# A hybrid decoder block: 32 tokens of the expert stage move from the dense path to the gathered path

## The chip, the core and the metric

The kernel runs on one core of a Trainium2 chip. The metric is the time of one execution on the device in microseconds (us), the median over several runs. TensorE (PE) multiplies, with its weight loads shown as PEld; VectorE (DVE), ScalarE (ACT) and GpSimd (POOL) do the elementwise work; SyncE (SP) issues the plain transfers; POOL issues the indirect ones. Each engine works through its own instructions in a fixed order that is settled when the kernel is compiled.

## What is computed

One decoder layer over 1024 tokens of width 1024: a combined projection, a gated DeltaNet and a sliding-window attention, an output projection, then PEER (retrieval of single-neuron experts), then a gated per-layer embedding and a final norm. The change touches PEER alone:

```
qry   = (ht @ wq)                        # 8 heads, two halves of 128
top_s, top_i = top_k(qry . sub_keys, 16)
best_s, expert = the 16 best of the 256 sums, per head   # 128 experts per token
gates = softmax(best_s)
act   = gelu(sum_d h[t, d] * u_tab[expert[t, k], d])
y[t]  = sum_k gates[t, k] * act[t, k] * v_tab[expert[t, k]]
```

There are 16384 experts; each token uses 128 of them (8 heads of 16).

## The kernel before

The tokens are cut into 8 blocks of 128. Their experts are computed in two ways, side by side in time.

**Dense path** (`DBLK`, blocks 0 to 4, 640 tokens; `dense`, from L922). All 16384 experts are multiplied with all tokens of these blocks, in 128 chunks `c` of 128 experts. For a chunk, `prepared` loads `ur` and `vr` and splits each into a high and a low part (`uh`, `ul`, `vh`, `vl`; ACT takes the high part, DVE the low one). Then, for each of two parts of 320 tokens, 8 x 3 matmuls fill a bank `bk_u` (tag "u", 2 banks); ACT turns it into `ge` (L988), DVE multiplies it with the gate table `Gt`, ACT and DVE split the product into `wh` and `wl`. After 4 chunks (one `cg`, 32 of them), the second product follows: for each of the 5 blocks and 2 halves of the width, 12 matmuls of 512 columns. Blocks 0 and 1 keep their sums in four banks "yp" through the whole stage; blocks 2 to 4 use the tag "y" with 2 banks, taken in turn, and DVE adds each bank to `xB` before the bank is free again. The gate table in DRAM (`gd`) was written earlier by `gbuild`.

**Gathered path** (`ABLK`, blocks 5 to 7; `gather_block`, L874). One partition is one token. For each of the 128 slots, POOL issues an indirect DMA (`fetched`, L858) that brings one row of `u` for each of 128 tokens, and DVE forms the dot product with `h2n` (`gather_dots`, L868). After the gelu, 128 more slots bring rows of `v`, and DVE adds each, scaled, to `acc` (L82). The landing tiles `rows` are a ring of 7 (`GBUF` 4 and `GXBUF` 3). The three blocks have 3 x 2 x 128 = 768 such steps.

What sets the order of the two: `step` in `dense` is called after each chunk and each (block, half), 448 times, and lets the gather job emit its share of the steps; `held_back` ties each gather instruction on DVE behind the third-last such point. Beyond that, a scheduler places the instructions of each engine by its own model when the program is built.

**Final stage** (`final`, L1002): per block a norm, eight transposes and 48 matmuls of 512 columns on `bk_g`, a gate, a last norm and the store, in the order 5, 6, 0, 1, 2, 3, 4, 7. Blocks 5 to 7 are read back from `x1d`, where the gathered path leaves them.

Of the kernel before, what the change touches and what calls it, by code (L numbers as in the profile page):

```python
# [7 lines left out]
F32 = mybir.dt.float32  # L8
# [22 lines left out]
ABLK = [5, 6, 7]  # L31
UBLK = HBLK + ABLK
BBLK = HBLK + DBLK
NU = len(DBLK) * 128
GC = 4
TB = 16
GBUF = 4
# [30 lines left out]
def block_kernel(ctx: ExitStack, tc, I, out, dbg=None):  # L68
    nc = tc.nc
    V, S, G, PE = nc.vector, nc.scalar, nc.gpsimd, nc.tensor  # L70
    NB = len(BBLK)
    NT = NB * P
    NH = len(HBLK) * P

    def copy(o, i, **k):
# [36 lines left out]

    ident = cp.tile([P, P], F32, name="ident")
    iota = cp.tile([P, P], F32, name="iota")
    sel_b = cp.tile([P, 3, 16, 8], BF, name="sel_b")
    mhalf = cp.tile([P, 8], F32, name="mhalf")
    G.memset(mhalf, -0.5)
# [10 lines left out]
    def load_consts():  # L128
        nc.sync.dma_start(ident, I["consts"][:, 0:P])
        nc.sync.dma_start(iota, I["consts"][:, 4 * P:5 * P])  # L130
        nc.sync.dma_start(cst, I["consts"][:, P:])
        V.tensor_copy(sel_b.rearrange("p s a h -> p (s a) h"), bc(sel[:, 58:106], 2, 8))
        V.memset(negt, NEG)
# [249 lines left out]
    def retrieving(lt, es):  # L383
# [14 lines left out]
        def retrieve(gi):  # L398
# [26 lines left out]
            for bi, b in enumerate(grp):  # L425
                xt = xts[bi]
                bs_ = slice(bi * P, (bi + 1) * P)
                nc.sync.dma_start(x1d[b], xt)
                h = norm(sm, "h", xt, ffnw, 1)
                if b in UBLK:  # L430
                    nc.sync.dma_start(h2d[UBLK.index(b)], h)
                transpose_split("s3", h, h2h, h2l, bs_)
                if b in DBLK:
                    t0 = (b - DBLK[0]) * P
                    nc.sync.dma_start(h2Td[0][:, :, t0:t0 + P], h2h.bitcast(F32)[:, :, bs_])
                    nc.sync.dma_start(h2Td[1][:, :, t0:t0 + P], h2l.bitcast(F32)[:, :, bs_])
            tv = [lt.tile([P, 16, 16], F32, tag="tv", name="tv", bufs=2) for _ in grp]
            tiu = [lt.tile([P, 16, 16], U32, tag="tiu", name="tiu", bufs=2) for _ in grp]
            for q4 in range(4):
# [317 lines left out]
    def topk(tk, bg, b, v, iu):  # L757
# [61 lines left out]
            stt(eidx[:, UBLK.index(b)], i1, 128.0, i2, ALU.mult, ALU.add)  # L819
        if b in ABLK:  # L820
            return
        pt = bank("gm", [4, P])
        tr(pt[:, 0], i1)
        tr(pt[:, 1], i2)
# [11 lines left out]

    def gbuild(bg, b):
        tT = slots[b]
        for tb in range(P // TB):
            stage = bg.tile([P, NE, TB], F32, tag="stage", name="stage", bufs=2)  # L840
            for t0 in range(0, TB, 4):
                c0 = tb * TB + t0
                o12 = bg.tile([P, 2, 4, P], F32, tag="o12", name="o12", bufs=2)
                o1, o2 = o12[:, 0], o12[:, 1]
                tt(o12, bc(bc(iota, 1, 4), 1, 2), bc(tT[:, 0:2, c0:c0 + 4], 3, P), ALU.is_equal)
                for i in range(4):
                    copy(o2[:, i], o2[:, i], scale=tT[:, 2, c0 + i:c0 + i + 1])
                pg = bank("gm", [4, P])
                for i in range(4):
                    mm(pg[:, i], o2[:, i], o1[:, i])  # L850
                copy(stage[:, :, t0:t0 + 4], pg.rearrange("p t e -> p e t"))
                yield
            nc.sync.dma_start(gd[:, :, BBLK.index(b) * (P // TB) + tb].rearrange("g p c t -> p g (c t)"),
                              stage.rearrange("p (g c) t -> p g (c t)", c=GC))

    def fetched(gp, tab, u, s):
        r = (pools["gx"] if "gx" in pools and s % 2 else gp).tile([P, D], F32, tag="rows", name="rows")
        G.indirect_dma_start(out=r, out_offset=None, in_=tab,  # L858
                             in_offset=bass.IndirectOffsetOnAxis(ap=eidx[:, u, s:s + 1], axis=0))
        return r  # L860

    def gather_dots(gp, u):
# [38 lines left out]
    pools = {}  # L901
    credit = [0.0]

    def gather_job():
        for b in ABLK:
            yield from gather_block(pools["gp"], b)

# [16 lines left out]
    def dense(xB):  # L924
        with ExitStack() as es:
# [12 lines left out]
            nparts = (NU + 511) // 512  # L938
            width = (NU // nparts + TB - 1) // TB * TB
            parts = [(n0, min(width, NU - n0)) for n0 in range(0, NU, width)]  # L940
            total = len(ABLK) * 2 * P
            steps = NE + NE // GC * NB * 2
            count = [0, 0]
            pools["job"] = gather_job()
# [22 lines left out]
            for cg in range(NE // GC):  # L967
# [30 lines left out]
                for bi in range(NB):  # L998
                    for j in range(2):
# [2 lines left out]
                        py = held[bi, j] if keep else bank("y")  # L1002
                        for ci in range(GC):
                            (vh, vl), (wh, wl) = vs[ci], ws[ci]
                            ts_ = slice(bi * P, (bi + 1) * P)
                            mm3(py, wh[:, ts_], wl[:, ts_], vh[:, cs], vl[:, cs],
                                ci == 0 and (cg == 0 or not keep), ci == GC - 1 and (cg == NE // GC - 1 or not keep))
                        if not keep or cg == NE // GC - 1:
                            last = tt(xB[:, bi, cs], py, xB[:, bi, cs], ALU.add)
                        step(last)  # L1010
            drain()

# [64 lines left out]
def _host(inputs):  # L1077
# [8 lines left out]
    wo_s = wo[512:].reshape(2, 4, 64, 1024).transpose(1, 0, 2, 3).reshape(512, 1024)  # L1086
    d = {
        "consts": _consts(),
        "x": a["x"][0],
        "pos": a["positions"][0].reshape(8, 128).T,  # L1090
        "mix_norm": a["mix_norm"][0],
# [42 lines left out]
```

## Time and profile before

| | |
|---|---|
| median of 3 runs (lowest, highest) | 3034.56 us (3032.35, 3036.15) |
| the profiled execution | 3043.6 us, span 3041.8 us |
| PE busy in the span | 2936.2 us, 97% |
| DVE busy | 2499.4 us, 82% |
| ACT busy, POOL busy | 1234.6 us, 1068.4 us |
| HBM read, written | 766.40 MB, 99.61 MB |
| moved by POOL's queue | 402.70 MB |

The span runs from the first to the last instruction. "Busy" is the time in which at least one instruction of the engine is under way; for PE the instructions overlap, so that what a matmul costs is read from the distance between two starts and not from its duration. "PEclk" is the granted clock of TensorE as a share of 2.4 GHz; "DMA share" is the mean busy share of the core's 16 DMA engines.

### The profile page before, as it was taken

The numbers are of one execution on the slowest core, as the hardware profiler recorded it, in microseconds if no ns is written. First come the engines' busy times: TensorE is split into PE (matmuls) and PEld (weight loads), VectorE is DVE, ScalarE is ACT, GpSimd is POOL, SyncE is SP. The second block draws the span as 40 slices with busy tenths as digits, with TensorE's granted clock in tenths as the row PEclk, the third lists the DMA queues.
The fourth block names the chain that finished last, engine by engine and source line by source line (L and its number), as shares of the span: only waits on it lengthen the run. The fifth ranks groups of instructions, "written<-read, shape, count | busy, mean of one in ns | idle before, by whom it ended". The sixth has DMA issues, their size and how long they took to land. (4 is left out here: it accounts for less than half of the span.)

```text
span 3041.8 us, 49726 instructions
## 1 busy us (share of the span) xinstructions
PE 2936.2 (97%) x18287; PEld 2690.0 (88%) x18287; DVE 2499.4 (82%) x5023; ACT 1234.6 (41%) x2761; POOL 1068.4 (35%) x901
## 2 busy tenths in 40 slices
PE   7999999999999889999999999999999999999988
PEld 5887999999998789999999989998898898998967
DVE  5658636898999779988699889887998898899974
ACT  5556634488777663222222222232232232222223
POOL 0000000000000000765356556554656565556541
PEclk9989999999999999999999999999999999999989
DMA  7569657689889994999799989888999899899962
GB/s 236 142 223 364 206 191 248 215 223 243 237 242 270 287 279 141 351 338 348 272 342 354 330 319 369 329 332 300 335 351 345 318 358 332 306 337 347 324 256 89
DMA packets 449955, 869.30 MB, mean 286 GB/s; under 512 B 193456, under 2 KB 235824, under 8 KB 445360
## 3 DMA queue, kind: packets, MB, share of 16 engines
q1 hardware_dynamic: 339120, 463.43, 46.5%
q0 software_dynamic: 110592, 402.70, 36.4%
q8 instruction: 143, 2.34, 0.3%
q14 instruction: 100, 0.82, 0.1%
HBM read 766.40 MB, written 99.61 MB: 285 GB/s over the span
## 5 line engine op out<-in xcount | busy, mean ns | idle before, releaser
L136 PE MATMUL bk_u<-hT,uh 128*128 128x320 f32 x4096 | 915.4, 310 | 7.0 <-DMA hT<-h2Td 3.7
L136 PEld LDWEIGHTS bk_u<-hT,uh 128*128 128x128 f32 x4096 | 695.7, 189 | 23.2 <-ACT ge L988 4.6
L858 POOL DMA_INDIRECT rows<-in_u_dram,eidx x384 | 499.1, 1300 | 555.5 <-DVE dots L868 283.1
L136 PE MATMUL bk_u<-hT,ul 128*128 128x320 f32 x2048 | 635.0, 310 | 0.3 <-DVE ul L79 0.3
L858 POOL DMA_INDIRECT rows<-in_v_dram,eidx x384 | 498.6, 1298 | 350.1 <-DVE acc L82 287.5
L82 DVE SCALAR_TENSOR_TENSOR acc<-rows,dots,acc 128x1024 f32<-128x1024 f32 x384 | 492.2, 1282 | 35.4 <-DMA rows<-in_v_dram,eidx 24.5
L868 DVE CUSTOM_DVE_ANT_0 rows<-rows,h2n 128x1024 f32<-128x1024 f32 x384 | 459.9, 1223 | 27.5 <-DMA rows<-in_u_dram,eidx 27.3
L136 PEld LDWEIGHTS bk_u<-hT,ul 128*128 128x128 f32 x2048 | 386.5, 189 | 4.1 <-DVE ul L79 0.7
L988 ACT ACTIVATE ge<-bk_u 128x320 f32<-128x320 f32 x256 | 109.8, 431 | 603.3 <-PE bk_u L136 552.6
L136 PE MATMUL bk_y<-vh,wh 128*128 128x512 f32 x768 | 298.9, 391 | 3.0 <-DVE xB L79 3.0
L136 PE MATMUL bk_y<-vl,wh 128*128 128x512 f32 x768 | 299.9, 392 | 0.0
L136 PE MATMUL bk_y<-vh,wl 128*128 128x512 f32 x768 | 296.8, 393 | 2.6 <-DVE wl L79 2.6
L76 ACT ACTIVATE wh<-ge 128x320 fp32r<-128x320 f32 x256 | 118.7, 469 | 316.7 <-DVE ge L79 304.1
L76 ACT ACTIVATE o<-o,tT 128x128 f32<-128x128 f32 x640 | 204.5, 392 | 56.4 <-DVE o L79 55.1
L76 ACT ACTIVATE uh<-ur 128x1024 fp32r<-128x1024 f32 x128 | 135.3, 1057 | 226.4 <-PE bk_u L136 217.5
L136 PE MATMUL bk_gm<-o 128*128 128x128 f32 x1280 | 203.2, 286 | 22.5 <-ACT o L76 16.2
L136 PE MATMUL bk_s<-h,whi 128*128 128x256 f32 x1024 | 209.1, 295 | 3.3 <-DMA whi<-wqc 1.0
L79 DVE TENSOR_TENSOR o<-iota,tT 128x1024 f32<-128x1024 f32 x160 | 194.7, 1220 | 11.5 <-PE bk_gm L136 8.9
L136 PEld LDWEIGHTS bk_gm<-o 128*128 128x128 f32 x1280 | 178.2, 195 | 29.0 <-ACT o L76 20.2
L136 PE MATMUL bk_yp<-vl,wh 128*128 128x512 f32 x512 | 199.7, 391 | 0.0
L136 PE MATMUL bk_yp<-vh,wh 128*128 128x512 f32 x512 | 199.1, 391 | 0.0
L79 DVE TENSOR_TENSOR xB<-bk_y,xB 128x512 f32<-128x512 f32 x192 | 131.1, 689 | 79.5 <-PE bk_y L136 79.1
(302 smaller groups left out, 5840.5 us busy)
## 6 DMA issues: line engine op xcount, KB each, us to landing
ur<-in_uT_dram SPq DMA_DIRECT2D x128, 512.0 KB, 6.8
vr<-in_v_dram SPq DMA_DIRECT2D x128, 512.0 KB, 6.7
gd<-stage SPq DMA_DIRECT2D x40, 1024.0 KB, 7.3
Gt<-gd SPq DMA_DIRECT2D x32, 1280.0 KB, 9.6
wlo<-wqc SPq DMA_DIRECT2D x128, 256.0 KB, 4.6
whi<-wqc SPq DMA_DIRECT2D x128, 256.0 KB, 4.7
whi<-woc SPq DMA_DIRECT2D x64, 256.0 KB, 4.8
wlo<-woc SPq DMA_DIRECT2D x64, 256.0 KB, 4.7
```

What stands on the lines that cost most here:

```text
L76: return S.activation(o, i, AF.Copy, **k)
L79: return V.tensor_tensor(o, a, b, op)
L82: return V.scalar_tensor_tensor(o, a, s, b, op0, op1, **k)
L136: PE.matmul(o, l, r, start=start, stop=stop)
L858: G.indirect_dma_start(out=r, out_offset=None, in_=tab, in_offset=bass.IndirectOffsetOnAxis(ap=eidx[:, u, s:s + 1], axis=0))
L868: held_back(V.tensor_tensor_reduce(out=r, in0=r, in1=h2n, op0=ALU.mult, op1=ALU.add, scale=1.0, scalar=0.0, accum_out=dots[:, s:s + 1]))
L988: S.activation(ge, pa, AF.Gelu_apprx_tanh)
```

## The change

The last 32 tokens of block 4 leave the dense path (`CUT = 32`, `NU` and `NT` become 608). The two parts of the first product have 304 columns in place of 320, the last block's second product has 96 rows in place of 128, and `Gt`, `hT` shrink in proportion. The 32 tokens are gathered: 4096 rows of `u` and as many of `v`, laid out with each token on four partitions of 32 slots each, so that 2 x 32 indirect DMAs of 128 rows bring them. Their indices and gates go through DRAM (`peidx`, `pegate`) into that layout (`pidx`, `pgate`). The four partial sums of a token are added by two matmuls with a 0/1 matrix `fold`, which use the banks "y", and DVE adds the result to `xB`. This job, `gather_part`, runs ahead of blocks 5 to 7.

```diff
-NU = len(DBLK) * 128
+CUT = 32
+NU = len(DBLK) * 128 - CUT
...
-    NT = NB * P
+    NT = NB * P - CUT
+    LB = DBLK[-1]
+    LP = P - CUT
...
+                if b == LB:
+                    nc.sync.dma_start(ph2d, h[LP:P, :])
...
+        if b == LB:
+            pe = tk.tile([P, P], I32, tag="pe", name="pe")
+            stt(pe, i1, 128.0, i2, ALU.mult, ALU.add)
+            nc.sync.dma_start(peidx, pe[LP:P, :])
+            nc.sync.dma_start(pegate, ga[LP:P, :])
+            for g in range(P // CUT):
+                nc.sync.dma_start(pidx[g * CUT:(g + 1) * CUT, :], peidx[:, g * CUT:(g + 1) * CUT])
+                nc.sync.dma_start(pgate[g * CUT:(g + 1) * CUT, :], pegate[:, g * CUT:(g + 1) * CUT])
...
+    def gather_part():
+        gp = pools["gp"]
+        h2n = gp.tile([P, D], F32, tag="hacc", name="h2n", bufs=1)
+        for g in range(P // CUT):
+            nc.sync.dma_start(h2n[g * CUT:(g + 1) * CUT, :], ph2d)
+        dots = gp.tile([P, P], F32, tag="dots", name="dots", bufs=1)[:, 0:CUT]
+        for s in range(CUT):
+            r = fetched(gp, I["u"], None, s)
+            held_back(V.tensor_tensor_reduce(out=r, in0=r, in1=h2n, op0=ALU.mult, op1=ALU.add, scale=1.0,
+                                             scalar=0.0, accum_out=dots[:, s:s + 1]))
+            yield
+        S.activation(dots, dots, AF.Gelu_apprx_tanh)
+        tt(dots, dots, pgate, ALU.mult)
+        acc = gp.tile([P, D], F32, tag="hacc", name="acc", bufs=1)
+        for s in range(CUT):
+            v = fetched(gp, I["v"], None, s)
+            if s == 0:
+                held_back(V.tensor_scalar(acc, v, dots[:, 0:1], None, op0=ALU.mult))
+            else:
+                held_back(stt(acc, v, dots[:, s:s + 1], acc, ALU.mult, ALU.add))
+            yield
+        xB = pools["xB"]
+        for j in range(2):
+            cs = slice(j * 512, (j + 1) * 512)
+            py = bank("y")
+            mm(py, fold, acc[:, cs])
+            tt(xB[:, len(DBLK) - 1, cs], py, xB[:, len(DBLK) - 1, cs], ALU.add)
+
     def gather_job():
+        yield from gather_part()
         for b in ABLK:
             yield from gather_block(pools["gp"], b)
...
-            total = len(ABLK) * 2 * P
+            total = len(ABLK) * 2 * P + 2 * CUT
...
-                            ts_ = slice(bi * P, (bi + 1) * P)
-                            mm3(py, wh[:, ts_], wl[:, ts_], vh[:, cs], vl[:, cs],
+                            ts_ = slice(bi * P, min((bi + 1) * P, NT))
+                            mm3(py[0:ts_.stop - ts_.start], wh[:, ts_], wl[:, ts_], vh[:, cs], vl[:, cs],
```

The compiled order of the changed program shows the following at three places. Line numbers there are those of the changed file.

PE, in the third group of chunks (`cg` 2), where the two fold matmuls stand; 720 of the matmuls on `bk_u` and 300 on `bk_y` and `bk_yp` stand ahead of them, and the second product of the dense path right behind:

```order
L141 MATMUL bk_u<-hT_13647,uh 128x304
L141 MATMUL bk_u<-hT_13646,ul 128x304
L141 MATMUL bk_y<-acc,fold 128x512 x2
L141 MATMUL bk_y<-vh,wh 128x512
L141 MATMUL bk_y<-vl,wh 128x512
```

In the kernel before, nothing but matmuls of the dense path stands in this stretch.

DVE, at the same place of the program: `L935` is the dot product of the 32 tokens, `acc` its second half, `L891` the dot product of block 5. Ahead of the first row stand 31 of the 32 dot products of the 32 tokens; between the first of them and the row of 31 stand 6 `ul`, 4 `vl`, 12 `ge`, 10 `wl` and 3 `xB`.

```order
L82 TENSOR_TENSOR ul<-ur,uh 128x1024
L935 ISA rows,dots<-rows,h2n 128x1024
L935 ISA dots 128x1
L82 TENSOR_TENSOR dots<-dots,pgate 128x32
L944 TENSOR_SCALAR acc<-rows,dots 128x1024
L85 SCALAR_TENSOR_TENSOR acc<-rows,dots,acc 128x1024 x31
L82 TENSOR_TENSOR xB<-bk_y,xB 128x512 x3
L891 ISA rows,dots<-rows,h2n 128x1024
```

Before, at the 32nd gather step, the order has one to three gather instructions at a time between those of the dense path. Now 31 stand together; behind them come 14 dot products and 7 `xB` (two of them those of the fold) before the next two `wl`.

DVE, at the end of the program. Before, eight `acc` follow the last `xB<-bk_y` of the dense path, and the order ends so:

```order
L79 TENSOR_TENSOR xB<-bk_y,xB 128x512
L82 SCALAR_TENSOR_TENSOR acc<-rows,dots,acc 128x1024 x5
L82 SCALAR_TENSOR_TENSOR h<-xt,rs,ple_norm 128x1024
...
L79 TENSOR_TENSOR xt<-gt,xt 128x512
L82 SCALAR_TENSOR_TENSOR h<-xt,rs,final_norm 128x1024
```

Now 64 `acc` follow the last `xB<-bk_y`; 47 of them lie among the instructions of `final`, and 17 behind the last norm of block 4:

```order
L82 TENSOR_TENSOR xB<-gt,xB 128x512
L85 SCALAR_TENSOR_TENSOR acc<-rows,dots,acc 128x1024 x3
L85 SCALAR_TENSOR_TENSOR h<-xB,rs,final_norm 128x1024
L85 SCALAR_TENSOR_TENSOR acc<-rows,dots,acc 128x1024 x17
L85 SCALAR_TENSOR_TENSOR h<-xt,rs,ple_norm 128x1024
L82 TENSOR_TENSOR hl<-bk_tp,hh 128x512 x2
```

Only the norm of block 7 (`h<-xt,rs,ple_norm`), its transposes and its 48 matmuls come after them.

## Rows read from the trace of the kernel before

**Rows 1.** Windows: us, busy us of each engine (instructions), PEclk, DMA share, GB/s.
```profile
1200.00:2900.00 1700.00, 1690.38 (x9454) 1537.55 (x9453) 1491.13 (x2070) 450.57 (x734) 974.44 (x751) 1.00 0.91 331
1250.00:1300.00 50.00, 50.00 (x285) 45.78 (x285) 44.22 (x77) 12.55 (x22) 34.20 (x25) 1.00 1.00 385
```
**Rows 2.** Timeline of PE, matmuls of 320 and 512 columns: start, us, engine, what.
```profile
1155.69 0.31 PE L136 MATMUL bk_u<-hT,ul 128*128 128x320 f32 x1
...
1156.13 0.31 PE L136 MATMUL bk_u<-hT,ul 128*128 128x320 f32 x1
...
2919.30 0.39 PE L136 MATMUL bk_y<-vh,wl 128*128 128x512 f32 x1
...
2919.99 0.39 PE L136 MATMUL bk_y<-vh,wl 128*128 128x512 f32 x1
```
**Rows 3.** Matmuls up to 1222.6 us, one window each for bk_u, bk_y and bk_yp.
```profile
0.00:1222.60 1222.60, 62.10 (x384) 59.91 (x384) 6.80 (x16) 0.98 0.77 235
...
0.00:1222.60 1222.60, 21.38 (x88) 16.45 (x89) 4.95 (x7) 0.98 0.77 235
...
0.00:1222.60 1222.60, 23.48 (x96) 17.74 (x96) 0.00 (x0) 0.98 0.77 235
```
**Rows 4.** Timeline of DVE, the first gather instructions.
```profile
1222.59 1.21 DVE L868 CUSTOM_DVE_ANT_0 rows<-rows,h2n 128x1024 f32<-128x1024 f32 x1
...
1224.87 1.22 DVE L868 CUSTOM_DVE_ANT_0 rows<-rows,h2n 128x1024 f32<-128x1024 f32 x1
```
**Rows 5.** Timeline of DVE, end of the dense path.
```profile
2921.41 0.68 DVE L79 TENSOR_TENSOR xB<-bk_y,xB 128x512 f32<-128x512 f32 x1
2922.01 3.92 DVE L82 SCALAR_TENSOR_TENSOR acc<-rows,dots,acc 128x1024 f32<-128x1024 f32 x3
2928.95 2.60 DVE L82 SCALAR_TENSOR_TENSOR acc<-rows,dots,acc 128x1024 f32<-128x1024 f32 x2 [3.02 <-DMA rows<-in_v_dram,eidx]
```
**Rows 6.** Groups of DVE by form: busy us, mean ns of one | idle before.
```profile
L79 DVE TENSOR_TENSOR ge<-ge,Gt 128x320 f32<-128x320 f32 x256 | 124.3, 490 | 39.4 <-ACT ge L988 25.0 <-DMA Gt<-gd 14.2
```
**Rows 7.** POOL's indirect DMAs: ns min/median/max; then its timeline.
```profile
L858 POOL DMA_INDIRECT rows<-in_v_dram,eidx x384: 932/1017/2625, 1449.0 to 2924.9; - x192
...
2905.84 1.49 POOL L858 DMA_INDIRECT rows<-in_v_dram,eidx  x1 [0.30 <-issue]
...
2922.61 1.49 POOL L858 DMA_INDIRECT rows<-in_v_dram,eidx  x1 [0.30 <-issue]
```
**Rows 8.** Timeline of DVE in the final stage, last norms of blocks 4 and 7.
```profile
3025.81 1.29 DVE L82 SCALAR_TENSOR_TENSOR h<-xB,rs,final_norm 128x1024 f32<-128x1024 f32 x1 [2.18 <-POOL rs L157]
3036.68 1.28 DVE L82 SCALAR_TENSOR_TENSOR h<-xt,rs,final_norm 128x1024 f32<-128x1024 f32 x1 [2.18 <-POOL rs L157]
```
**Rows 9.** Block 7 from its last gather step: SP, its transfers' landing, ACT, DVE, last matmul.
```profile
2939.84 0.33 SPq L884 DMA_DIRECT2D x1d<-acc  x1
2942.47 0.33 SPq L1036 DMA_DIRECT2D xt<-x1d  x1
...
DMA to landing us min/median/max: 3.2/7.3/11.4
...
2987.61 1.08 ACT L190 ACTIVATE h<-xt 128x1024 f32<-128x1024 f32 x1
...
2989.71 1.28 DVE L82 SCALAR_TENSOR_TENSOR h<-xt,rs,ple_norm 128x1024 f32<-128x1024 f32 x1 [0.43 <-POOL rs L157]
...
3032.03 0.39 PE L136 MATMUL bk_g<-wgh,hl 128*128 128x512 f32 x1
```
**Rows 10.** PE after its idle stretch: timeline, and two windows (PEclk third from the end).
```profile
2932.81 1.97 PE L139 MATMUL bk_tp<-ident,h 128*128 128x128 f32 x8 [12.44 <-DVE h L82]
2934.61 0.79 PE L136 MATMUL bk_g<-wgh,hh 128*128 128x512 f32 x1
...
2932.80:2936.00 3.20, 3.19 (x11) 2.73 (x12) 3.20 (x3) 1.78 (x3) 0.00 (x0) 0.50 0.31 87
2936.00:2945.00 9.00, 7.61 (x35) 5.89 (x34) 9.00 (x11) 6.07 (x11) 2.47 (x6) 0.72 0.57 197
```

More of the change, by code (lines that the diff above doesn't have):

```diff
@@ L114, in block_kernel @@
     iota = cp.tile([P, P], F32, name="iota")
+    fold = cp.tile([P, P], F32, name="fold")
     sel_b = cp.tile([P, 3, 16, 8], BF, name="sel_b")
@@ L130, in load_consts @@
         nc.sync.dma_start(iota, I["consts"][:, 4 * P:5 * P])
+        nc.sync.dma_start(fold, I["fold"])
         nc.sync.dma_start(cst, I["consts"][:, P:])
@@ L149, in block_kernel @@
     gd = dr.tile([NE // GC, P, NT // TB, GC, TB], F32, name="gd")
+    pidx = cp.tile([P, CUT], I32, name="pidx")
+    pgate = cp.tile([P, CUT], F32, name="pgate")
+    peidx = dr.tile([CUT, P], I32, name="peidx")
+    pegate = dr.tile([CUT, P], F32, name="pegate")
+    ph2d = dr.tile([CUT, D], F32, name="ph2d")
     eidx = cp.tile([P, len(UBLK), P], I32, name="eidx")
@@ L432, in retrieve @@
                 transpose_split("s3", h, h2h, h2l, bs_)
+                if b == LB:
+                    nc.sync.dma_start(ph2d, h[LP:P, :])
                 if b in DBLK:
                     t0 = (b - DBLK[0]) * P
-                    nc.sync.dma_start(h2Td[0][:, :, t0:t0 + P], h2h.bitcast(F32)[:, :, bs_])
-                    nc.sync.dma_start(h2Td[1][:, :, t0:t0 + P], h2l.bitcast(F32)[:, :, bs_])
+                    n = LP if b == LB else P
+                    ns = slice(bi * P, bi * P + n)
+                    nc.sync.dma_start(h2Td[0][:, :, t0:t0 + n], h2h.bitcast(F32)[:, :, ns])
+                    nc.sync.dma_start(h2Td[1][:, :, t0:t0 + n], h2l.bitcast(F32)[:, :, ns])
             tv = [lt.tile([P, 16, 16], F32, tag="tv", name="tv", bufs=2) for _ in grp]
@@ L838, in gbuild @@
         tT = slots[b]
-        for tb in range(P // TB):
+        for tb in range((LP if b == LB else P) // TB):
             stage = bg.tile([P, NE, TB], F32, tag="stage", name="stage", bufs=2)
@@ L858, in fetched @@
         G.indirect_dma_start(out=r, out_offset=None, in_=tab,
-                             in_offset=bass.IndirectOffsetOnAxis(ap=eidx[:, u, s:s + 1], axis=0))
+                             in_offset=bass.IndirectOffsetOnAxis(
+                                 ap=pidx[:, s:s + 1] if u is None else eidx[:, u, s:s + 1], axis=0))
         return r
@@ L940, in dense @@
             parts = [(n0, min(width, NU - n0)) for n0 in range(0, NU, width)]
-            total = len(ABLK) * 2 * P
+            total = len(ABLK) * 2 * P + 2 * CUT
+            pools["xB"] = xB
             steps = NE + NE // GC * NB * 2
@@ L1004, in dense @@
                             (vh, vl), (wh, wl) = vs[ci], ws[ci]
-                            ts_ = slice(bi * P, (bi + 1) * P)
-                            mm3(py, wh[:, ts_], wl[:, ts_], vh[:, cs], vl[:, cs],
+                            ts_ = slice(bi * P, min((bi + 1) * P, NT))
+                            mm3(py[0:ts_.stop - ts_.start], wh[:, ts_], wl[:, ts_], vh[:, cs], vl[:, cs],
                                 ci == 0 and (cg == 0 or not keep), ci == GC - 1 and (cg == NE // GC - 1 or not keep))
                         if not keep or cg == NE // GC - 1:
-                            last = tt(xB[:, bi, cs], py, xB[:, bi, cs], ALU.add)
+                            np_ = min(P, NT - bi * P)
+                            last = tt(xB[0:np_, bi, cs], py[0:np_], xB[0:np_, bi, cs], ALU.add)
                         step(last)
@@ L1088, in _host @@
         "consts": _consts(),
+        "fold": ((np.arange(P)[None, :] >= P - CUT)
+                 & (np.arange(P)[:, None] % CUT == np.arange(P)[None, :] % CUT)).astype(np.float32),
         "x": a["x"][0],
```

## The prediction

> **What bounds the kernel now.** I read the windows first. From 1200 to 2900 us PE is busy 1690 of 1700 us, at full clock; DVE is busy 1491 us (88%) and the DMA engines 0.91 [rows 1]. So the dense stage is PE's, but DVE and the DMA engines have little room: in the fullest 50 us the DMA share is 1.00, at 385 GB/s. I then read the distance between starts of matmuls. Of 320 columns, three take 0.44 us, 0.147 each; of 512, three take 0.69 us, 0.23 each [rows 2]. Next the places where the gathered path begins and ends on DVE: its first instruction starts at 1222.59 us [rows 4], and the last `xB<-bk_y` at 2921.41, with eight accumulations behind it [rows 5]. The final stage lasts 120.4 us from there to the end of the span. PE works through its blocks one after another: the last norms of blocks 4 and 7 are 10.9 us apart [rows 8]. Block 7, gathered last, is early enough there to cost nothing.
>
> The sum below is made against the profiled execution's own 3043.6 us. The median of the runs is 3034.6, 9 us lower; I take the 9 us off at the end. A measurement of this kernel tells about 0.2% (6 us) from no change.
>
> **Part 1, fewer columns.** 128 chunks x 2 parts x 24 = 6144 matmuls go from 320 to 304 columns. A column costs (0.23 - 0.147) / 192 = 0.43 ns [rows 2]. That is 6.8 ns for 16 columns, hence 0.140 us each, and 6144 x 6.8 ns = **42 us** less on the engine that bounds (37 to 47, for a hundredth of a us either way in the 0.23). The second product still streams 512 columns; its 96 output rows save nothing there. DVE's 512 `ge` and `wl` shrink by a twentieth of 490 ns [rows 6] at most, 12 us off DVE, and each load of `Gt` by 64 KB. Neither bounds, so I count neither.
>
> **Part 2, the wait for the fold.** The two fold matmuls stand in PE's order with 720 matmuls on `bk_u` and 300 on `bk_y` and `bk_yp` ahead of them, and PE passes nothing over them. When DVE reaches its first gather instruction, PE has done 384 and 184 of these [rows 3]. It still has 336 x 0.140 = 47.0 us and 116 x 0.23 = 26.7 us of work, and so comes to the fold 73.7 us later. The fold needs all 64 new steps on DVE. I assume that DVE starts them where it starts gathering now, since in both orders the same work of the upstream stages precedes.
>
> DVE's time to that point: 32 dot products at 1.14 us (two in 2.28) [rows 4], 36.5 us; 32 accumulations, 31 of them unbroken, at 1.31 (three in 3.92) [rows 5], 41.9 us; between them 6 `ul` and 4 `vl`, which are as wide as an accumulation, at 1.28, 12 `ge` and 10 `wl` at 0.47, and 3 `xB` at 0.68, less the 0.08 us by which neighbours overlap [rows 5, 6], 22 us. Sum 101 us. The DMA engines' time: POOL's queue moved 402.70 MB in 768 steps, 0.52 MB a step; 64 steps are 33.6 MB, the dense loads of seven chunks and one or two `Gt` 9.5 MB, less some five steps that land ahead as now; 40.5 MB at 385 GB/s [rows 1] make 105 us. These two overlap, each with gaps the other doesn't have; I take 107. PE waits 107 - 73.7 = 33 us. Then DVE is behind: 14 dot products and 7 `xB` (20 us) stand before the next two `wl`, while PE has five groups of 12 matmuls (13.8 us) for it; 6 us more. With the two fold matmuls and the clock after an idle stretch, **40 us**. The lower bound is DVE's sum alone and no lag, 27; the upper one is rival D's.
>
> What waits behind: the dense path's second product uses the banks "y" in turn, so nothing on them can pass the fold, and `wh` and `wl` have five buffers, so the first product stops as well. After the fold DVE has fewer gather steps left per matmul than before (704 for the rest of the stage against some 715), so the rest stays PE's, and Part 1's gain holds there.
>
> By the Trainium skill's page "GPSIMD Engine Reference", section 1 (Specifications), GpSimd shares its SBUF interfaces with VectorE and contends with DVE instructions of two SBUF inputs; both kinds of gather instruction on DVE are that. What such a block would cost here is rival D, whose 131 us of issues would stand in place of my 107 and add 24 us to this part.
>
> **Part 3, the end.** Now 64 accumulations, not 8, follow the last `xB<-bk_y`, and block 7 can start only behind the last. DVE's sum: 64 x 1.28 = 82 us [rows 5], and the final stage's other work for seven blocks, 14 each of `gt`, `hl` and the gate's add, of 512 columns, at 0.68 [rows 5], 14 norms and eight `wgl` of 1024 at 1.28 [rows 8], 57 us; less 7 us for neighbours' overlap, 131 us. By PE instead: the last norm of block 4 starts 104.4 us after that `xB` today [rows 5, 8]; with 17 x 1.31 behind it, 128 us. So both lie close together; with waits for rows like the 3.02 us one [rows 5], 136 us.
>
> Then block 7's chain. From the last accumulation the store and reload take 2.6 + 3.2 us [rows 9]; ACT's square to the start of DVE's norm 2.1 (2987.61 to 2989.71); the norm 1.28 [rows 9] and from the first transpose to the first matmul 1.8 (2932.81 to 2934.61, behind a like idle stretch) [rows 10]. 48 matmuls x 0.23 make 11.0 us. PE has stood idle some 30 us by then; after 12.4 us idle its granted clock today is 0.50, the lower level of 1.2 GHz, and the mean of 0.72 in the 9 us after 2936 means 5 us more at it [rows 10]; of these 6.4 us with matmuls half is lost, 3 us. From the last matmul to the end of the span 9.8 [rows 9]. Sum 34.8 us.
>
> So the end lasts 136 + 35 = 171 us where it lasts 120.4: **51 us more**. Lower bound 128 + 32 (full clock) gives 40; upper, ten more waits of 1.5 us, 65.
>
> **Small edits, counted at nothing.** 19 new transfers on SP (the constant, `ph2d`, the indices and gates and their copies, `h2n`): the reload of the indices waits on their store, some 3 us each way, counted by the 2.6 us of a store today [rows 9]; they stand in SP's order beside the loads of `hT`, long ahead of the first gather, and hide there; without that cover 6 us, inside the range. The added index instruction on DVE is of 128 columns. `xB` for 96 partitions costs what 128 do.
>
> **Sum.** 3043.6 - 42 + 40 + 51 = 3092.6; less 9, **3083 us**.
>
> **Rivals.**
> A. Faster: PE's columns are all that counts. DVE has 209 idle us in 1200 to 2900 [rows 1], and 64 steps need 82. Were they spread evenly, PE would never wait and the gather would end where it ends now: 3034.6 - 42 = 2993. This decides if the fold is ready before PE's 73.7 us are over and no more than some 20 steps are left at the end. The fixed order speaks against both.
> B. The fold's wait is covered and only the end counts: -42 + 51, 3044.
> C. The end is hidden and only the fold counts: -42 + 40, 3033. It needs block 7's rows some 45 us earlier than the order puts them.
> D. POOL cannot issue while DVE runs an instruction of this kind: each issue waits out one of 1.28 us and takes its own 0.93 [rows 5, 7], 2.2 us, so 59 issues take 131 us. Part 2 becomes 64 (57 of wait, 7 as above), and the last 17 add 2: -42 + 64 + 53 = +75, 3109. For it: ten issues stand 1.86 us apart at the end of the dense path [rows 7]. Against it: the median issue takes 1.02 us, while DVE is busy 88% of the time. The page of the Trainium skill named in Part 2 states this kind of contention; the trace bears it out by half.
> E. The narrower matmuls cost what the wide ones do (the change does not do what it says): 3083 + 42 = 3125. The distance of 0.147 at 320 against 0.23 at 512 speaks against it [rows 2].
>
> **How the numbers follow.** Forecast 0.76, A 0.03, B 0.05, C 0.04, D 0.10, E 0.02. Faster is A, 0.03; within 0.2% is C, 0.04; the rest is slower, 0.93. All lower bounds together give 3034.6 - 47 + 27 + 40 = 3055, all upper ones without D 3034.6 - 37 + 40 + 65 = 3103; they will hardly fall together, so the range begins at 3058, and it runs to 3109 to take in D. A, B, C and E lie outside, 0.14.
>
> **What would show it.** Matmuls on `bk_u` 0.140 us apart. One idle stretch of PE of 25 to 45 us between 1280 and 1340, ended by DVE's `acc`, and then 31 accumulations in a row on DVE. The dense path's last matmul within 15 us of today's 2920. Sixty-four accumulations behind it, PE idle for 25 to 45 us before block 7's transposes, and the span's end 165 to 180 us behind the last `xB<-bk_y`. If PE shows no idle stretch at the fold, Part 2 is wrong; if block 7's matmuls follow block 4's at once, Part 3 is; if neither stretch is there and the time is near 2993, A was right.

## The result, and the profile after

The changed kernel takes **3169.10 us** (median of 4 runs, 3164.76 to 3183.88) where the kernel before takes 3035.36 us (median of 4, 3032.35 to 3037.89). The ratio is 1.0452, 95% interval 1.0422 to 1.0483: 134 us slower. Forecast were 3083 us, 48 us slower, with a range from 3058 to 3109. The sign was right, and the size was far off.

The profiled execution of the changed kernel takes 3183.88 us, its span 3182.1 us (before 3041.8). It is the longest of the four, 15 us above their median, so what is read from its span comes out high by up to that much. I cut both spans at the last matmul of the dense path. Before, it starts at 2919.99 us [rows 2], and 121.8 us follow. Now it starts at 2997.98 us, and 184.1 us follow. So 78 us are lost in dense, where the forecast had -42 + 40 = -2, and 62 us behind it, where it had 51. The surplus sits in dense.

The window over dense, to be read beside [rows 1] (the columns are the same):

```profile
1200.00:2900.00 1700.00, 1606.65 (x9041) 1419.25 (x9040) 1423.26 (x2028) 420.09 (x693) 1196.53 (x730) 0.98 0.87 320
```

PE is busy 84 us less than before, DVE 68 us less, and the DMA share fell from 0.91 to 0.87. Only POOL is busier, by 222 us, with fewer instructions. An engine that is off the critical path has become slow. What it does there is to issue indirect DMAs; below, an "issue" is one such instruction of POOL. The page's groups say where (group | busy us, mean ns of one | idle before):

```profile
L880 POOL DMA_INDIRECT rows<-in_u_dram,eidx x384 | 641.5, 1670 | 280.6 <-DVE dots L891 194.2
L880 POOL DMA_INDIRECT rows<-in_v_dram,eidx x384 | 626.0, 1630 | 242.5 <-DVE acc L85 156.2
L85 DVE SCALAR_TENSOR_TENSOR acc<-rows,dots,acc 128x1024 f32<-128x1024 f32 x415 | 530.9, 1279 | 107.1 <-DMA rows<-in_v_dram,eidx 94.6
```

And the view of POOL's line has the spread (ns min/median/max):

```profile
L880 POOL DMA_INDIRECT rows<-in_u_dram,eidx x384: 932/1222/16230, 1324.8 to 2844.0; - x192
L880 POOL DMA_INDIRECT rows<-in_v_dram,eidx x384: 932/1024/15642, 1595.7 to 3137.7; - x192
```

The median issue costs what it did, 1024 ns against 1017 [rows 7]. The longest takes 16.2 us where it took 2.6. Counted over the trace, 48 issues last over 2.2 us, and what they take above 1.3 us each adds up to 305 us; before, it was 5 issues and 6 us. One of them, on POOL's timeline:

```profile
1521.67 0.94 POOL L880 DMA_INDIRECT rows<-in_u_dram,eidx  x1 [0.31 <-issue]
1524.34 12.97 POOL L880 DMA_INDIRECT rows<-in_u_dram,eidx  x1 [1.73 <-DVE dots L891]
1537.61 0.94 POOL L880 DMA_INDIRECT rows<-in_u_dram,eidx  x1 [0.30 <-issue]
```

and what DVE does meanwhile:

```profile
1523.99 0.08 DVE L891 DVE_READ_ACCUMULATOR2_ANT dots<- 128x1 f32 x1
1523.99 0.68 DVE L82 TENSOR_TENSOR xB<-bk_y,xB 96x512 f32<-96x512 f32 x1
1524.59 1.21 DVE L82 TENSOR_TENSOR vl<-vr,vh 128x1024 fp32r<-128x1024 f32 x1
...
1535.28 1.22 DVE L82 TENSOR_TENSOR ul<-ur,uh 128x1024 fp32r<-128x1024 f32 x1
1541.57 1.22 DVE L891 CUSTOM_DVE_ANT_0 rows<-rows,h2n 128x1024 f32<-128x1024 f32 x1 [5.08 <-DMA rows<-in_u_dram,eidx]
```

The issue begins 0.35 us behind the start of an add on **96 partitions**. Until 1536.50 no instruction of DVE starts behind the end of the one ahead; then DVE has nothing left to do, and 0.8 us later, at 1537.31, the issue ends. By then the rows that had landed are used up, and DVE waits 5.08 us for new ones. Of the 32 issues over 2.7 us between 1240 and 2990 us, 25 end 0.4 to 0.8 us behind the beginning of a stretch in which DVE is idle. Of the other seven, four end 0.8 us behind the end of the next add on 96 partitions, and three at neither. The add on 96 partitions comes twice per group of chunks, and the long issues come about once per group.

In the kernel before, DVE has stretches as dense that do POOL no harm. From the first of these rows of DVE's timeline to the idle time ahead of the last, 50 us, every instruction of DVE starts before the one ahead has ended, and the 25 issues that begin in between take 1.95 us at most.

```profile
2417.78 1.23 DVE L868 CUSTOM_DVE_ANT_0 rows<-rows,h2n 128x1024 f32<-128x1024 f32 x1 [1.21 <-DMA rows<-in_u_dram,eidx]
...
2468.23 0.49 DVE L79 TENSOR_TENSOR ge<-ge,Gt 128x320 f32<-128x320 f32 x1 [0.27 <-ACT ge L988]
```

From POOL the delay reaches PE by way of DVE. Between 1340 and 2998 us DVE waits 192 us for gathered rows (in run 1 below, 29 us from 1340 to 2920), and the dense path's instructions behind them in DVE's order come late for PE, which waits 57 us in all (in run 1, 8). The view of waits has the largest (us in total, times, longest):

```profile
DVE rows L891 <- DMA rows<-in_u_dram,eidx: 101.8, 53, 7.1
DVE acc L85 <- DMA rows<-in_v_dram,eidx: 90.7, 31, 8.5
PE bk_y L141 <- DVE xB L82: 21.7, 15, 7.3
PE bk_yp L141 <- DVE wl L82: 14.5, 12, 4.6
PE bk_yp L141 <- ACT wh L79: 14.2, 8, 3.3
```

The terms that the forecast did have are there too. The matmuls on `bk_u` start 0.14 us apart (six distances in 0.83 us), and PE stands idle before the fold, for 48.65 us:

```profile
1284.72 0.30 PE L141 MATMUL bk_u<-hT,ul 128*128 128x304 f32 x1
1284.85 0.44 PE L141 MATMUL bk_u<-hT,uh 128*128 128x304 f32 x2
1285.13 0.30 PE L141 MATMUL bk_u<-hT,ul 128*128 128x304 f32 x1
1285.27 0.44 PE L141 MATMUL bk_u<-hT,uh 128*128 128x304 f32 x2
1285.55 0.30 PE L141 MATMUL bk_u<-hT,ul 128*128 128x304 f32 x1
1334.49 2.08 PE L141 MATMUL bk_y<-acc,fold 128*128 128x512 f32 x2 [48.65 <-DVE acc L85]
```

And before block 7's transposes PE stands idle for 43 us:

```profile
3155.54 1.94 PE L144 MATMUL bk_tp<-ident,h 128*128 128x128 f32 x8 [43.40 <-DVE h L85]
```

### The profile page after: what moved, and what is told of

Same layout as the page of the kernel before. It is cut to its first block, busy times and chain, and to the rows that moved or that the text cites. A ratio compares the mean times of both kernels' runs of the same rounds, so it can differ in the third digit from the quotient of the medians.

```text
span 3182.1 us, 49853 instructions
## 1 busy us (share of the span) xinstructions
PE 2925.8 (92%) x18227; PEld 2629.9 (83%) x18227; DVE 2560.4 (80%) x5115; ACT 1216.9 (38%) x2724; POOL 1426.6 (45%) x965
## 4 chain that ended last, share of the span: by engine, by line
PE 29%; issue 27%; DMA 15%; POOL 14%; DVE 11%; ACT 4%; SPq 0%; POOLq 0%; DVEq 0%; ACTq 0%
POOL rows L880 13%; PE bk_acc L141 6%; DMA rows<-in_v_dram,eidx 6%; PE bk_s L141 5%; DMA rows<-in_u_dram,eidx 4%; PE bk_u L141 4%; PE bk_y L141 3%; PE bk_dn L141 3%; PE bk_gm L141 2%; DVE acc L85 2%; PE bk_g L141 2%; DVE o L82 1%; PE bk_yp L141 1%; DVE rows L891 1%; PE bk_sw L141 1%
## 5 line engine op out<-in xcount | busy, mean ns | idle before, releaser
L141 PE MATMUL bk_u<-hT,uh 128*128 128x304 f32 x4096 | 872.5, 303 | 7.7 <-ACT ge L1041 3.9
L880 POOL DMA_INDIRECT rows<-in_u_dram,eidx x384 | 641.5, 1670 | 280.6 <-DVE dots L891 194.2
L880 POOL DMA_INDIRECT rows<-in_v_dram,eidx x384 | 626.0, 1630 | 242.5 <-DVE acc L85 156.2
L141 PE MATMUL bk_u<-hT,ul 128*128 128x304 f32 x2048 | 618.1, 302 | 0.0
L891 DVE CUSTOM_DVE_ANT_0 rows<-rows,h2n 128x1024 f32<-128x1024 f32 x384 | 460.5, 1218 | 107.7 <-DMA rows<-in_u_dram,eidx 101.8
L79 ACT ACTIVATE wh<-ge 128x304 fp32r<-128x304 f32 x256 | 115.1, 456 | 580.5 <-DVE ge L82 485.7
L141 PE MATMUL bk_y<-vh,wh 128*128 128x512 f32 (+1 forms) x768 | 308.6, 403 | 21.7 <-DVE xB L82 21.7
L1041 ACT ACTIVATE ge<-bk_u 128x304 f32<-128x304 f32 x256 | 106.4, 418 | 541.2 <-PE bk_u L141 449.4
L141 PE MATMUL bk_y<-vl,wh 128*128 128x512 f32 (+1 forms) x768 | 305.6, 399 | 0.0
L141 PE MATMUL bk_y<-vh,wl 128*128 128x512 f32 (+1 forms) x768 | 302.7, 399 | 3.1 <-DVE wl L82 3.1
L141 PE MATMUL bk_yp<-vh,wl 128*128 128x512 f32 x512 | 183.9, 400 | 14.6 <-DVE wl L82 14.5
```

What stands on the lines that cost most here:

```text
L79: return S.activation(o, i, AF.Copy, **k)
L141: PE.matmul(o, l, r, start=start, stop=stop)
L880: G.indirect_dma_start(out=r, out_offset=None, in_=tab, in_offset=bass.IndirectOffsetOnAxis(ap=pidx[:, s:s + 1] if u is None else eidx[:, ...
L891: held_back(V.tensor_tensor_reduce(out=r, in0=r, in1=h2n, op0=ALU.mult, op1=ALU.add, scale=1.0, scalar=0.0, accum_out=dots[:, s:s + 1]))
L1041: S.activation(ge, pa, AF.Gelu_apprx_tanh)
```

## The experiments

Three theories stood against each other for the 80 us that dense lost beyond the forecast. ROWS: the add on 96 partitions blocks POOL's gather issues. STEPS: 26 gather steps per group where there were 24 leave DVE no gaps. STALL: the 49 us at the fold put gathers and dense out of step.

Three words are used below. A "partial" instruction is one on fewer than 128 partitions, a "full" one is on all 128. A "stand" of DVE is time, however short, in which none of its instructions is under way; the timeline marks only longer ones in brackets, so short ones are read from starts and ends. Runs 5 and 7 to 10 are one execution each; the executions of each of the others lie within 19 us of each other. In the traces the order of the instructions on PE, DVE, ACT and POOL is the same in the changed kernel and run 1, in the kernel before and runs 2 and 5, in runs 3 and 4, and in runs 9 and 10, so no other order explains what differs there.

**1. The changed kernel with the add on 128 partitions.**

```diff
-ts_ = slice(bi * P, min((bi + 1) * P, NT))
+ts_ = slice(min(bi * P, NT - P), min((bi + 1) * P, NT))
-np_ = min(P, NT - bi * P)
+np_ = P
```

> The changed kernel, but the last dense block's second product takes 128 columns of weights (tokens 480 to 607) and its add into xB runs on all 128 partitions instead of 96. Left out by that: block 4's rows are not the right ones (the last 32 tokens of block 3 are added to its first rows). What moves is only the shape of 64 adds on VectorE and of their matmuls' weights; matmuls keep 512 columns. Theory ROWS (a gather's issue on POOL that meets the add on 96 partitions stays blocked until VectorE's stream has a gap): no gather issue over 3 us behind 1300 us (now 48 over 2.2 us, the longest 16.2), dense's last matmul some 50 to 60 us earlier than 2998, the time 3110 us (3095 to 3125). Theory STEPS (the long issues come from 26 gather steps per group of chunks where there were 24, and VectorE has no gaps left): over 40 long issues stay, time 3160 to 3180. Theory STALL (the 49 us that TensorE stands at the fold matmuls put the gathers out of step with dense): long issues stay, time 3160 to 3180.

Measured: 3109.07 us (ratio 1.0234, 1.0217 to 1.0252), 60 us less than the changed kernel, as ROWS expected. No issue is longer than 2.6 us, as the view of POOL's line in this run shows:

```profile
L880 POOL DMA_INDIRECT rows<-in_v_dram,eidx x384: 932/1017/2626, 1570.4 to 3061.5; - x192
```

And on its PE timeline dense's last matmul is where the kernel before has it, 78 us earlier than in the changed kernel's profiled execution and not 50 to 60:

```profile
2919.97 0.39 PE L141 MATMUL bk_y<-vh,wl 128*128 128x512 f32 x1
```

ROWS holds; STEPS and STALL fall, since steps and stall are still in this run (PE waits 45.16 us at the fold).

**2. The kernel before with the add on 96 partitions.** Nothing else is changed.

```diff
-last = tt(xB[:, bi, cs], py, xB[:, bi, cs], ALU.add)
+np_ = 96 if bi == NB - 1 else P
+last = tt(xB[0:np_, bi, cs], py[0:np_], xB[0:np_, bi, cs], ALU.add)
```

> The kernel before, in which only the add of the last dense block into xB is cut from 128 partitions to 96 (64 instructions); 32 tokens of that block are left out of the sum. ROWS: gather issues of 9 to 16 us appear, about one per group of chunks, and the time rises by 30 to 65 us, to 3065 to 3100. STEPS and STALL: no issue over 2.7 us, time 3030 to 3040 as before.

Measured: 3103.60 us, ratio 1.0193 (1.0161 to 1.0225). That is just above the expected range. 64 instructions that became smaller cost 66 us by themselves. POOL's line in this run:

```profile
L858 POOL DMA_INDIRECT rows<-in_v_dram,eidx x384: 932/1016/16560, 1463.6 to 2987.7; - x192
```

**3 and 4. Dense cut without the gather of the 32 tokens**, on 96 partitions and on 128 (the edit of 1).

```diff
-        yield from gather_part()
...
-            total = len(ABLK) * 2 * P + 2 * CUT
+            total = len(ABLK) * 2 * P
```

> The changed kernel without the gather of the 32 tokens (64 gather steps and the fold are gone; these 32 tokens lack their dense share), 608 tokens dense and the adds on 96 partitions kept. 24 steps per group of chunks as before, no wait at the fold. ROWS: long gather issues stay (30 or more over 5 us) and eat the gain of the shorter matmuls: 3045 us (3025 to 3070). STEPS: no long issues, 2993 us (the 42 us of Part 1 in full). STALL: the same 2993.

> As the run without the gather of the 32 tokens, and in addition the adds and the weights of the last block on 128 partitions (tokens 480 to 607), so that no instruction of dense runs on 96. Left out: the 32 tokens' share, and block 4's rows are wrong. ROWS: no gather issue over 3 us, time 2993 us (2985 to 3005), some 50 us less than its twin with 96 partitions. STEPS and STALL: equal to its twin within 5 us, both 2993. If neither reaches 2993, Part 1's 42 us are not TensorE's to give, and VectorE bounds dense.

Measured: 3071.22 us with 96 partitions (ratio 1.0105, 1.0088 to 1.0122), 3019.98 us with 128 (0.9933, 0.9914 to 0.9953). The 51 us between them are ROWS again. The first lies just above what ROWS expected, the second 27 us above 2993. By the text of the expectation, a time above 2993 in both would mean that Part 1's 42 us are not TensorE's to give. That does not follow: Part 1's gain does arrive in dense, where the last matmul on PE's timeline starts 43.2 us earlier than before.

```profile
2876.76 0.39 PE L141 MATMUL bk_y<-vh,wl 128*128 128x512 f32 x1
```

But 144.4 us follow it instead of 121.8. The order, which is fixed ahead, puts 44 accumulations behind the last dense add where it put 8. The gather stream did not become faster; a dense stage that is 43 us shorter leaves 36 steps behind.

**5. The kernel before with the add on 64 partitions** (the edit of 2 with 64).

> The kernel before, in which the add of the last dense block into xB runs on 64 partitions (64 tokens of the block are left out of the sum). If any add on fewer than 128 partitions blocks the gather issues: issues over 9 us appear as in the twin with 96, time 3090 to 3105. If 96 alone does it (a start or a count that is no power of two): no issue over 2.7 us, time 3030 to 3045.

Measured: 3110.15 us, with issues of up to 16.6 us. So 96 is not special.

**6. Block 4's product and add ahead of block 3's.**

```diff
-for bi in range(NB):
+for bi in [*range(NB - 2), NB - 1, NB - 2]:
```

> The changed kernel, adds on 96 partitions kept, but in each group of chunks the last block's product and add come ahead of block 3's, so that each add on 96 partitions is followed some 3 to 8 us later by one on 128 that reads PSUM too. The whole computation is kept. Theory ENDED BY A FULL ADD (a blocked gather issue goes on at VectorE's next gap or at the next add from PSUM on 128 partitions, whichever comes first): issues over 2.2 us stay as many, 40 to 60, but none over 9 us behind 1300 us; time 3120 to 3150. Theory GAP ONLY: issues of 12 to 16 us stay, time 3160 to 3180.

Measured: 3127.40 us (ratio 1.0303, 1.0286 to 1.0321), 42 us less than the changed kernel. 36 issues are over 2.2 us, three of them over 9 (the longest 12.5), so ENDED BY A FULL ADD held for a part only. Of the 22 issues over 2.7 us, eight end within 0.3 us of the end of the next full add, two 0.8 us behind the next add on 96 partitions, and twelve, the three longest among them, 0.4 or 0.8 us behind the beginning of a stand. Two of the three longest had lasted through a full add. Where a full add lets one issue through, the next can be blocked again. POOL's timeline in this run:

```profile
2048.08 7.83 POOL L880 DMA_INDIRECT rows<-in_u_dram,eidx  x1 [5.81 <-DVE dots L891]
2056.21 4.12 POOL L880 DMA_INDIRECT rows<-in_u_dram,eidx  x1 [0.30 <-DVE xB L82]
```

The first of these ends at 2055.91, the second at 2060.33 us. DVE's timeline has the two full adds there:

```profile
2055.41 0.68 DVE L82 TENSOR_TENSOR xB<-bk_y,xB 128x512 f32<-128x512 f32 x1
...
2059.43 0.68 DVE L82 TENSOR_TENSOR xB<-bk_y,xB 128x512 f32<-128x512 f32 x1
```

**7. Another instruction on 96 partitions.** In the kernel before, one in eight `wl<-ge,wh` is split into partitions 0 to 95 and 96 to 127.

```diff
+np_ = 96 if ci == GC - 1 and n0 else P
-last = tt(wl[:, m0:m0 + n], ge, wh[:, m0:m0 + n], ALU.subtract)
+last = tt(wl[0:np_, m0:m0 + n], ge[0:np_], wh[0:np_, m0:m0 + n], ALU.subtract)
+if np_ < P:
+    last = tt(wl[np_:P, m0:m0 + n], ge[np_:P], wh[np_:P, m0:m0 + n], ALU.subtract)
```

> The kernel before, in which one in eight of the subtractions wl<-ge,wh (the last chunk of a group, its second part; 32 instructions) is split into one on partitions 0 to 95 and one on 96 to 127; both read SBUF alone, and the whole computation is kept. If any instruction on fewer than 128 partitions blocks the gather issues: issues over 9 us, some 20 to 30 of them, time 3070 to 3110. If it must read PSUM, as the add into xB does: no issue over 2.7 us, time 3030 to 3055 (32 instructions more of 0.46 us).

Measured: 3034.71 us, the longest issue 3.2 us. Taken alone this spoke for PSUM; runs 8 to 10 show that it was the second half, or rather the stand behind it.

**8. A copy of one column on 96 partitions** behind each add of the last block in the kernel before.

```diff
+if bi == NB - 1:
+    last = V.tensor_copy(tiny[0:96], xB[0:96, bi, j * 512:j * 512 + 1])
```

> The kernel before, and behind each add of the last dense block a copy of one column of xB on 96 partitions into a tile that nobody reads (64 instructions; the whole computation is kept). If the count of partitions alone does it, however short the instruction and with one input in SBUF: issues over 9 us, 20 or more, time 3080 to 3110. If it takes a long instruction or two inputs: no issue over 2.7 us, time 3030 to 3050.

Measured: 3063.07 us, and seven issues over 6 us, the longest 14.3. The time lies between the two expectations. PSUM, two inputs and length are not needed; yet most of the 64 places let POOL through, and why is open. Nor need the copy come just ahead: the longest issue begins 10.7 us behind the last copy, after four of 0.9 to 2.1 us, with no stand of DVE in between. A place that does not let it through, on DVE's timeline of this run:

```profile
1933.30 0.14 DVE L1012 COPY tiny<-xB 96x1 f32<-96x1 f32 x1
1933.36 1.21 DVE L869 CUSTOM_DVE_ANT_0 rows<-rows,h2n 128x1024 f32<-128x1024 f32 x1
```

and on POOL's:

```profile
1933.57 12.23 POOL L859 DMA_INDIRECT rows<-in_u_dram,eidx  x1 [3.42 <-DVE tiny L1012]
```

**9 and 10. The add split in two, in both orders**, in the kernel before. The work is the same in both.

```diff
-last = tt(xB[:, bi, cs], py, xB[:, bi, cs], ALU.add)
+for p0, p1 in ([(0, 96), (96, P)] if bi == NB - 1 else [(0, P)]):
+    last = tt(xB[p0:p1, bi, cs], py[p0:p1], xB[p0:p1, bi, cs], ALU.add)
```

> The kernel before, in which each add of the last dense block is split in two that follow each other directly: partitions 0 to 95, then 96 to 127 (64 instructions of some 0.6 us more; the whole computation is kept). Theory LAST (the blocked issues depend on which partitions the last add leaves out, and one on 96 to 127 right behind it ends the blocking, as in the run in which a subtraction was split the same way and no issue was long): no issue over 3 us, time 3030 to 3060. Theory COUNT (each instruction from PSUM on fewer than 128 partitions blocks, whatever follows): issues over 9 us, 25 or more, time 3090 to 3140.

> The twin with the two halves the other way round: partitions 96 to 127 first, then 0 to 95; the whole computation is kept, and the work is the same. LAST: the add on 0 to 95 is the last again, so issues over 9 us, 25 or more, time 3090 to 3120. COUNT: the same as its twin within 15 us, both 3090 to 3140. If neither has long issues, splitting alone (two instructions back to back) undoes the blocking.

Measured: 3056.32 us with partitions 96 to 127 last, the longest issue 3.2 us; 3155.72 us with partitions 0 to 95 last, with 21 issues over 9 us. LAST had run 9 right and the long issues of run 10 too, whose time is 36 us above its range; COUNT falls. The order of two neighbours is worth 99 us. DVE's timeline shows one difference. In the first run both halves take 1.40 us, to 1694.16, and the next instruction starts 0.03 us behind their end:

```profile
1692.76 1.40 DVE L79 TENSOR_TENSOR xB<-bk_y,xB 96x512 f32<-96x512 f32 x2
1694.19 1.23 DVE L79 TENSOR_TENSOR vl<-vr,vh 128x1024 fp32r<-128x1024 f32 x1
```

In the second, 1.40 us from 1715.61 end at 1717.01, and the next instruction starts 0.08 us ahead of that; the issue that POOL begins at 1716.70 then takes 17.19 us:

```profile
1715.61 1.40 DVE L79 TENSOR_TENSOR xB<-bk_y,xB 32x512 f32<-32x512 f32 x2
1716.93 1.21 DVE L79 TENSOR_TENSOR vl<-vr,vh 128x1024 fp32r<-128x1024 f32 x1
```

This pair alone does not tell whether the 0.03 us lets POOL go on, or the partitions of the half that comes last. Another issue of run 10 does, on POOL's timeline and DVE's:

```profile
2789.01 8.18 POOL L858 DMA_INDIRECT rows<-in_v_dram,eidx  x1 [0.30 <-issue]
...
2795.11 1.27 DVE L82 SCALAR_TENSOR_TENSOR acc<-rows,dots,acc 128x1024 f32<-128x1024 f32 x1
2796.41 1.23 DVE L79 TENSOR_TENSOR vl<-vr,vh 128x1024 fp32r<-128x1024 f32 x1
```

DVE stands still from 2796.38 to 2796.41 us, between two full instructions and 7 us behind the last partial one, and 0.81 us behind the beginning of this stand the issue ends. In 26 more of the 54 issues over 2.7 us in this run the end lies 0.80 to 0.82 us behind the beginning of a stand of 0.03 us, there the one ahead of a half on 96 to 127. So a stand of 0.03 us is enough to let POOL go on. Where the stand at the halves comes from is stated by the Trainium skill's page "VectorE: DVE Perf Modes", section "Two Vector instructions with no wait between them": an instruction whose operand starts in another group of 32 partitions than the last one's in the same memory begins only when all earlier ones have finished. The rows of runs 9 and 10 agree with it (0.03 us behind, where the start moves back from 96 to 0; 0.08 us ahead, where it stays at 0). So does run 7, whose second half starts at 96 too; on DVE's timeline both halves end at 1278.16 us, and the next instruction starts 0.03 us behind:

```profile
1277.17 0.99 DVE L79 TENSOR_TENSOR wl<-ge,wh 96x320 fp32r<-96x320 f32 x2
1278.19 1.23 DVE L868 CUSTOM_DVE_ANT_0 rows<-rows,h2n 128x1024 f32<-128x1024 f32 x1
```

**11. Both faults out**, with the whole computation kept.

```diff
-wh = ap.tile([P, NT], F32R, tag="wh", name="wh", bufs=GC + 1)
-wl = ap.tile([P, NT], F32R, tag="wl", name="wl", bufs=GC + 1)
+wh, wl = padded[c % (GC + 1)]
-ts_ = slice(bi * P, min((bi + 1) * P, NT))
+ts_ = slice(bi * P, (bi + 1) * P)
-np_ = min(P, NT - bi * P)
+np_ = P
...
+nc.sync.dma_start(paccd, acc)
...
+if b == LB:
+    pa = fp.tile([P, D], F32, tag="xt", name="pa", bufs=3)
+    nc.sync.dma_start(pa, paccd)
+    for j in range(2):
+        cs = slice(j * 512, (j + 1) * 512)
+        py = bank("tp")
+        mm(py, fold, pa[:, cs])
+        tt(xt[:, cs], py, xt[:, cs], ALU.add)
```

`padded` are five pairs of tiles of 640 columns, whose last 32 are set to zero once.

> The changed kernel with both suspected faults out and the whole computation kept: the second factor wh, wl is padded with zeros to 640 columns, so that the last block's product and its add run on 128 partitions, and the fold is not on TensorE's way in dense: the accumulation of the 32 tokens goes to DRAM and is folded and added just before block 4's gate in the final stage. Expected by all: no gather issue over 3 us, no idle stretch of TensorE over 6 us between 1250 and 1400 us, dense's last matmul at 2870 to 2885 us. Theory SATURATED (the gather stream already does all the steps that VectorE has time for while dense runs: 759 of 768 in the kernel before, 767 of 832 in the run with 128 partitions, both with dense's last matmul at 2920.0 us): the 45 us that TensorE gains turn into about 35 more accumulations behind dense, 95 to 105 instead of 65, and the time falls by 5 to 15 us only, to 3095 to 3105. Theory STOOD (the wait at the fold is lost time of the whole kernel): about 65 accumulations behind dense as before, the time 3060 to 3070.

Measured: 3117.36 us (ratio 1.0272, 1.0255 to 1.0289). Dense ends 48.9 us earlier than in run 1, at 2871.12, and the time is 8 us longer. STOOD falls. SATURATED had the 104 accumulations and the place of dense's end right, and the time is 12 us above its range: 244.9 us follow dense now instead of 186.4. On PE's timeline the wait before block 7's transposes has grown to 86.78 us:

```profile
3089.48 1.97 PE L144 MATMUL bk_tp<-ident,h 128*128 128x128 f32 x8 [86.78 <-DVE h L85]
```

**12. The same with eight row buffers** (`GXBUF = 4`).

> The run with both faults mended, with four instead of three row buffers in the second pool, eight in all instead of seven; the order that is fixed ahead then leaves 91 accumulations behind dense instead of 104. Theory BUFFERS (the gather stream is paced by its row buffers and the order made for them; in the mended run a step behind dense took (3078.9 - 2871.1) / 104 = 2.0 us): the 13 steps fit into dense without cost, time 3117 - 26 = 3091 (3083 to 3100). Theory SUM (VectorE and the transfers are full in dense, so 13 steps more push dense back by what they save behind it): time 3108 to 3120, dense's last matmul 5 to 20 us later than 2871.

Measured: 3089.88 us (ratio 1.0176, 1.0156 to 1.0196). BUFFERS holds: 27 us for one more buffer, with dense's end unmoved at 2867.90 us. This is the best version that does the whole computation with 608 tokens dense, and it is still 54 us slower than the kernel before. No run points to one that beats both kernels; eight row buffers in the kernel before were not tried.

## Why the prediction was right or wrong

Read in spans of the profiled executions, the runs split the change into three steps:

| | last dense matmul | behind it | span |
|---|---|---|---|
| before | 2920.0 | 121.8 | 3041.8 |
| run 4: dense cut alone | 2876.8 | 144.4 | 3021.2 |
| run 1: with the 32 tokens gathered | 2920.0 | 186.4 | 3106.4 |
| the changed kernel: add on 96 partitions | 2998.0 | 184.1 | 3182.1 |

- **Part 1 was right.** Forecast 42 us, measured 43.2 (run 4), with the matmuls 0.14 us apart.
- **Part 2 was right in mechanism, and the wait itself 12 us short.** Forecast 40 us: a wait of 33, a lag of 6. Measured: a wait of 45.2 us in run 1 and 48.65 in the changed kernel; for dense as a whole 43.2 us (run 4 to run 1) or 48.9 (run 11 to run 1). In run 1, PE is ahead of the place that I took from the kernel before when DVE starts to gather (399 and 208 matmuls done, not 384 and 184) and comes to the fold 66.3 us later, not 73.7; DVE has the 64 steps done after 111.4 us, not 107.
- **Part 3 was right in mechanism, and 14 us short.** The 64 accumulations are there, and PE waits before block 7. The end behind the last matmul grew by 64.6 us in run 1, forecast 51. The term that was mis-sized is the 136 us from the last `xB<-bk_y` to the last accumulation's end: run 1 has 148.2 (2921.48 to 3069.71). Block 7's chain took 36.7 us, forecast 34.8. DVE's work up to there was as summed, 131.7 us against 131, but I allowed 5 us of idle time, and it was 16. The window over that stretch of run 1 (its third busy time is DVE's):

```profile
2920.00:3068.00 148.00, 90.46 (x394) 70.79 (x392) 131.66 (x130) 37.63 (x62) 105.51 (x88) 0.84 0.83 292
```

- **The step that failed** stands among the edits counted at nothing: "`xB` for 96 partitions costs what 128 do." For DVE it does, 0.68 us. For POOL it doesn't: it cost 76 us of span (60 in the medians, run 1 to the changed kernel), and 66 us set into the kernel before (run 2). With it fell the sentence of Part 2 by which Part 1's gain holds in the rest of dense. In the kernel before, every instruction of DVE in the dense stage is on 128 partitions, so its rows could show no gather beside a partial one. This was a cost to bound from both sides, and I did not even name it as unknown.
- **Rival D** had the right engine and the wrong trigger. It made every issue wait out one instruction of DVE with two SBUF inputs, 2.2 us each. Measured, the median issue stayed at 1.02 to 1.22 us, and a few, behind a partial instruction, waited, most of them until DVE stood still. The Trainium skill's "GPSIMD Engine Reference", section 1 (Specifications), names two SBUF inputs as a cause of contention. The rows bear out that VectorE can hold POOL up, but with full-width instructions alone the longest issue of the kernel before and of run 1 took 2.6 us, 1.7 us above the shortest; the large price needs a partial instruction ahead.
- **Rivals A, B and C** fell on the stated points: the fold came before its steps were done, and 64 steps were left. Rival E fell with the 0.14 us.
- Of the stated marks, the idle stretch at the fold (48.65 us, up to 45 stated), the end behind the last `xB` (183.3 us, up to 180) and the place of the last dense matmul (2998, 2920 stated) were missed; the last is the one that told of the failed step.

Why the trade did not pay even without the partial add: PE was busy 99% of dense, but DVE 88% and the DMA engines 0.91 [rows 1], and with seven row buffers the order had just fitted the gather steps into dense's time. Cutting dense by 43.2 us left 36 of them behind (run 4), by 48.9 us left 40 more than in run 1 (run 11): one step for each 1.2 us of dense. The change takes from the engine with the longest work and adds 64 steps to a stream that was full.

## What to carry to other kernels

When a tile's rows become fewer than 128, look at POOL in the trace, not at the engine that runs the smaller instruction: if indirect DMAs are issued beside a busy VectorE, pad the rows to 128 (run 11), or let an instruction that starts at another group of 32 partitions follow (run 9, which still paid 22 us for its 64 added instructions). When work is moved off the bounding engine, count what its receiver has left in the same stretch, row buffers included. An edit that "costs nothing" wants a bound like any other when its form occurs nowhere in the trace.

## What the runs showed of the hardware

- A VectorE instruction on partitions 0 to 95 or 0 to 63 can block POOL's indirect DMAs behind it, for up to 17.2 us. Over all fourteen traces there are 186 issues of more than 3.3 us, and each begins behind such an instruction (run 8: one of a single column; run 10: half of a split add) in a stretch in which VectorE has worked without a stand since. 145 of them end 0.4 or 0.8 us behind the beginning of a stand, and none lasts through one. Of the other 41, 30 end near the next add from PSUM, at most 0.9 us behind its end; for 11 the end is not explained.
- With full-width instructions alone the longest issue was 2.6 us in the kernel before and in runs 1, 4 and 11, and 3.2 us in run 12. In the kernel before, POOL issued 25 times at up to 1.95 us through 50 us in which VectorE had no stand at all.
- 0.03 us of standing were enough (the rows of run 10; and runs 9 and 10, 3056 against 3156 us for the same two instructions in either order).
- Not settled: what inside the engines holds the issue, why some issues behind a partial instruction pass all the same (most of them in run 8), and whether partial instructions of other engines, or of VectorE on other partitions than the first ones, do it, which was not tried.
